# A mixture-of-experts block on one core: 280 tokens by dense products instead of 288, 104 tokens by gathered rows instead of 96

## The chip, the cores and the metric

The kernel runs on one NeuronCore of a Trainium2 chip. The metric is the device time of one execution in microseconds (us), taken as the median of several executions. A profile of one execution comes with it; its span runs from the first to the last instruction on the core.

The engines in the text: PE is the matrix engine (its weight loads are listed as PEld), DVE the vector engine, ACT the activation engine, POOL the general engine that here issues gathers and small copies, SP the engine that issues most loads. Each engine executes its own instructions in the order in which they stand, and waits on semaphores for the others.

## The reference

One transformer block on 512 tokens of width 2048: a mixer (chunked linear memory, forgetting attention, gated merge), cross attention over 256 memory rows, and an expert layer, each followed by a residual and a layer norm. The change lies in the expert layer:

```
q = (x @ w_pq).reshape(B, S, PEER_HEADS, 2, PEER_DK // 2)
sc = jnp.einsum('bshpd,hpnd->bshpn', q, sub_keys)          # 128 keys per half
top_s, top_i = lax.top_k(sc, PEER_TOPK)                    # 16 per half
best_s, best_pos = lax.top_k(cand_s, PEER_TOPK)            # 16 of the 256 pairs, per head
idx, g = take_along_axis(cand_i, best_pos), softmax(best_s)
# per token: 8 heads x 16 = 128 experts out of 16384
a = einsum('tkd,td->tk', expert_u[idx], x);  hact = gelu(a) * g
out = einsum('tk,tkd->td', hact, expert_v[idx])
x = layer_norm(DN_ALPHA * x + out, ln_w[2], ln_b[2])
```

An expert's number is 128 times its key in the first half plus its key in the second. So the 16384 experts are 128 groups ("keys") of 128.

## The kernel before, in words

All products are made in float32 accuracy from three products of split operands: a tile `w` becomes `whi` (a cast on ACT, L133) and `wlo = w - whi` (a subtraction on DVE, L134), and `whi*xhi + whi*xlo + wlo*xhi` are summed in PSUM (`products`, L201). Every weight tile of 128 x 1024 floats is loaded by SP (`load_raw`, L145), cast and subtracted. Two rings of buffers hold them in the expert layer, together six raw tiles, five `whi` and five `wlo`.

The mixer, the cross attention and the queries come first and are not changed. Token block 0 (128 tokens) has its experts done by gathering from an earlier point on. The blocks 1 to 3 are divided: the first 288 of their 384 tokens are dense, the last 96 gathered.

Dense tokens. For each key `c` of 128, `stage_a(c)` multiplies the 128 experts' `u` rows of that key with all dense tokens (two weight tiles, 48 products with 288 columns each) and applies gelu on ACT (tile `ga`). For each group of eight keys (`c0`, `J = 8`), `stage_o(c0, q)`, q = 0 to 3, multiplies the gated activations with the `v` rows of these keys (sixteen weight tiles a group, 24 products each, four PSUM banks `po`), and DVE adds the banks to `acc` (L1422). Between the two, `stage_h(c)` multiplies `ga` by the gate tile `G` (L1313) and splits the result into `hph` and `hpl`.

The gates are dense too: `G` says for every expert of a key and every token what weight the token gives it, mostly zero. It is built ahead in rounds of four tokens ("gate rounds" below): DVE makes two one-hot tiles `o` (L1244), ACT scales one of them token by token (four instructions, L1249), PE multiplies them (four products, L1250), and ACT copies the bank into four `stage` tiles (four copies, L1253). After 12 rounds (`GB = 48` tokens) the stage tiles are written to DRAM (`gd`, four DMAs issued by ACT, L1255). There are 72 rounds. `stage_h` reads `G` back for four keys at a time, so the first `stage_o` cannot begin before the last round is in DRAM. The rounds themselves wait for the selection of the top 16 (`select`, DVE).

`LOOK = 76` keys of `stage_a` run before the first `stage_o`; the other 52 are spread evenly over the groups. 126 of the 128 activations go to DRAM (`gad`, ACT queue) and come back (`gb`, SP queue); the text of the code calls them `spilled`.

Gathered tokens. `gathered(t, r0, n, ...)` takes n tokens; each holds 128/n partition rows, so that 128 experts are fetched at a time: n gathers from `u`, each followed by a product with the token's row and a sum (L929, DVE), then gelu and gates, then n gathers from `v`, each followed by a multiply-add into `xacc` (L932, DVE). A product with a 0/1 matrix folds the 128/n rows of a token (four products and copies, L950, L951). Each step is a job; `EARLY = 44` of the 194 jobs run beside the first 76 keys, the others at an even rate up to the group of key 112. A job waits for a given weight tile's split (`after`, "pace"). Each part ends with its own layer norm: two broadcast loads of norm weights, statistics, `rstd`, four DVE instructions (L964 to L983).

The end. In the last group, after each q, PE turns `acc` into token rows (`turned_out`, L1358), statistics are gathered, and after q = 3 `last_rows` finishes the norm of three blocks of dense tokens (128, 128 and 32) and writes them.

The order of instructions on each engine is not as written: a scheduler with a model of the durations lays it out when the program is built, and the built order of any version can be read. PE therefore has gate rounds, `stage_a` and `stage_o` interleaved in an order that is fixed before it runs.

## Time and profile before

| | us |
|---|---|
| median of three runs | 4829.66 |
| lowest and highest | 4826.51, 4833.37 |
| profiled execution | 4827.06 |
| its span | 4825.3 |
| PE busy | 4695.9 |
| DVE busy | 3736.9 |
| ACT busy | 2203.7 |
| first `stage_a` product | 3065.2 |
| first and last gate product | 3363.1, 3581.6 |
| first `stage_o` product | 3617.7 |
| last `stage_o` product | 4804.7 |

A row of a group or a timeline gives the source line, the engine, the operation, what is written from what and the tile's shape; in brackets or behind a bar stands how long the engine was idle before it and what ended that. "PE 120.00 (x906)" in a table of stretches means 120.00 us busy and 906 instructions that touch the stretch.

### The profile page before, as it was taken

To read this page: it belongs to the slowest core of one execution; us is meant where nothing else is said; L and a number is where in the kernel's file an instruction comes from. 1 tells how busy PE (TensorE), PEld (TensorE's weight loads), DVE (VectorE), ACT (ScalarE), POOL (GpSimd) and SP (SyncE) were. 2 spreads that over 40 slices of the span, in tenths; PEclk is the share of its full clock that TensorE was granted. 3 is DMA by queue.
4 is the path that set the end of the run, shared out by engine and by line. 5 is a ranking of instruction groups with operands and counts; after the bars stand their busy time and mean duration, and the time that the engine had idled before them with its cause. 6 is when DMAs were issued, how large, how long until landed. Compare 5 with 4: busy or idle time off the path is not lost. (4 is left out here: it accounts for less than half of the span.)

```text
span 4825.3 us, 75381 instructions
## 1 busy us (share of the span) xinstructions
PE 4695.9 (97%) x28720; PEld 4343.2 (90%) x28720; DVE 3736.9 (77%) x5326; ACT 2203.7 (46%) x3388; POOL 932.2 (19%) x884
## 2 busy tenths in 40 slices
PE   7999999999999899999989999999999999999999
PEld 6889788887888899999988779999999999999998
DVE  7776677766699777888769586899877888888886
ACT  6665666555543223343332334444874333343333
POOL 0000111200002332333334120111101222221110
PEclk9999999999999999999999999999999999999999
DMA  7888999865669899998889585588789999999993
GB/s 263 287 287 294 316 333 326 283 218 190 194 202 356 326 363 342 340 333 327 303 306 383 196 307 185 201 289 285 275 309 353 347 349 352 351 333 348 364 360 121
DMA packets 384380, 1435.00 MB, mean 297 GB/s; under 512 B 44412, under 2 KB 109676, under 8 KB 325392
## 3 DMA queue, kind: packets, MB, share of 16 engines
q1 hardware_dynamic: 268176, 832.52, 49.2%
q0 software_dynamic: 91456, 556.10, 30.8%
q10 hardware_dynamic: 24384, 41.56, 2.3%
q8 instruction: 225, 3.69, 0.3%
q14 instruction: 139, 1.14, 0.1%
HBM read 1338.10 MB, written 91.76 MB: 296 GB/s over the span
## 5 line engine op out<-in xcount | busy, mean ns | idle before, releaser
L134 DVE TENSOR_TENSOR wlo<-raw,whi 128x1024 fp32r<-128x1024 f32 x1472 | 1782.0, 1220 | 746.3 <-ACT whi L133 512.9
L133 ACT CAST whi<-raw 128x1024 fp32r<-128x1024 f32 x1472 | 1527.9, 1052 | 1710.7 <-PE mm L201 878.0
L201 PE MATMUL po<-hph,whi 128*128 128x288 f32 x2048 | 551.2, 296 | 9.9 <-ACT whi L133 9.9
L201 PE MATMUL sm<-Ch,whi 128*128 128x288 f32 x2048 | 557.8, 298 | 2.4 <-ACT whi L133 1.3
L201 PE MATMUL sm<-Cl,whi 128*128 128x288 f32 x2048 | 556.7, 296 | 0.0
L201 PE MATMUL po<-hpl,whi 128*128 128x288 f32 x2048 | 551.0, 296 | 0.5 <-DVE hpl L134 0.5
L901 POOL DMA_INDIRECT rows<-in_peer_u,eid x224 | 324.1, 1447 | 1173.5 <-DVE rows L929 486.8
L932 DVE SCALAR_TENSOR_TENSOR xacc<-rows,dots,xacc 128x2048 f32<-128x2048 f32 x224 | 525.4, 2345 | 21.6 <-DMA rows<-in_peer_v,eid 20.1
L901 POOL DMA_INDIRECT rows<-in_peer_v,eid x224 | 369.4, 1649 | 872.4 <-DVE xacc L932 464.4
L929 DVE SCALAR_TENSOR_TENSOR rows<-rows,xacc 128x2048 f32<-128x2048 f32 x224 | 511.3, 2285 | 24.1 <-DMA rows<-in_peer_u,eid 23.2
L201 PE MATMUL mm<-xh,whi 128*128 128x384 f32 x1280 | 437.7, 344 | 7.2 <-ACT whi L133 4.2
L201 PE MATMUL mm<-xl,whi 128*128 128x384 f32 x1280 | 430.9, 338 | 0.0
L201 PEld LDWEIGHTS po<-hph,whi 128*128 128x128 f32 x2048 | 383.9, 189 | 12.0 <-ACT whi L133 11.1
L201 PEld LDWEIGHTS sm<-Ch,whi 128*128 128x128 f32 x2048 | 384.9, 188 | 4.1 <-ACT whi L133 2.4
L201 PEld LDWEIGHTS po<-hpl,whi 128*128 128x128 f32 x2048 | 383.8, 189 | 2.4 <-issue 1.7
L201 PEld LDWEIGHTS sm<-Cl,whi 128*128 128x128 f32 x2048 | 385.0, 188 | 0.0
L201 PE MATMUL po<-hph,wlo 128*128 128x288 f32 x2048 | 337.9, 297 | 2.6 <-DVE wlo L134 2.5
L201 PE MATMUL sm<-Ch,wlo 128*128 128x288 f32 x2048 | 327.4, 298 | 1.1 <-DVE wlo L134 1.0
L201 PEld LDWEIGHTS po<-hph,wlo 128*128 128x128 f32 x2048 | 294.1, 189 | 7.1 <-DVE wlo L134 5.3
L201 PEld LDWEIGHTS sm<-Ch,wlo 128*128 128x128 f32 x2048 | 288.5, 188 | 3.8 <-DVE wlo L134 2.8
L201 PE MATMUL mm<-xh,wlo 128*128 128x384 f32 x1280 | 255.1, 335 | 0.0
L201 PEld LDWEIGHTS mm<-xh,whi 128*128 128x128 f32 x1280 | 242.2, 189 | 14.3 <-ACT whi L133 4.5
(440 smaller groups left out, 8527.7 us busy)
## 6 DMA issues: line engine op xcount, KB each, us to landing
raw<-in_w_in SPq DMA_DIRECT2D x512, 512.0 KB
raw<-in_uT SPq DMA_DIRECT2D x256, 512.0 KB
raw<-in_vq SPq DMA_DIRECT2D x256, 512.0 KB
raw<-in_w_xkv SPq DMA_DIRECT2D x64, 512.0 KB
raw<-in_w_br_ml SPq DMA_DIRECT2D x64, 512.0 KB
raw<-in_w_br_fx SPq DMA_DIRECT2D x64, 512.0 KB
raw<-in_w_out SPq DMA_DIRECT2D x64, 512.0 KB
raw<-in_peer_wq SPq DMA_DIRECT2D x64, 512.0 KB
```

The source lines that it names most:

```text
L133: nc.scalar.copy(hi, src)
L134: return nc.vector.tensor_sub(lo, src, hi.bitcast(F32))
L201: nc.tensor.matmul(o, w if stat else x, x if stat else w, start=k == first and x is xh and not part, stop=k == last and part == 1)
L901: i = nc.gpsimd.indirect_dma_start(out=rows, out_offset=None, in_=I[table], in_offset=bass.IndirectOffsetOnAxis(ap=ei[:, k:k + 1], axis=0))
L929: after(nc.vector.scalar_tensor_tensor(rows, rows, 1.0, xacc, op0=ALU.mult, op1=ALU.mult, accum_out=dots[:, k:k + 1]), last())
L932: after(nc.vector.scalar_tensor_tensor(xacc, rows, dots[:, k:k + 1], xacc, op0=ALU.mult, op1=ALU.add), last())
```

## The change

Seven things go together.

1. `NDENSE` is 280: every product, gelu, gate, split and add of the dense stages has 280 columns instead of 288, and there are 70 gate rounds in five groups of 14 (`GB = 56`).
2. The gathered tokens are 104, in three parts of 64, 32 and 8. The third part brings 16 gathers with 16 DVE instructions, four folding products and copies, and, since each of its tokens has 16 partition rows, 32 small copies of indices and gates and 16 small loads of its token rows on POOL.
3. `LOOK` is 72 and `EARLY` 56: 56 jobs run beside the first 72 keys.
4. The other 56 keys of `stage_a` are no longer spread evenly. The groups of keys 0 to 56 do none; each group from key 64 to 112 does the eight keys of the next group, two beside each q, and `stage_h` of a key follows its `stage_a` at once.
5. The activations of these 56 keys stay in SBUF; 72 activations go through DRAM instead of 126.
6. The remaining 155 jobs run 6 or 7 to a group up to the group of key 56, and 16 or 17 to a group from key 64 to key 104. The last two groups have none.
7. The three gathered parts no longer make their own norm. Each writes its rows to DRAM (`yg`), they are read back as one tile of 104 rows, and `gathered_rows` makes one norm for them in the last group, after q = 1.

```diff
-NDENSE = 288
-GATHERED = ((64, 64), (32, 32))
-GB = 48
+NDENSE = 280
+GATHERED = ((64, 64), (32, 32), (24, 8))
+GB = 56
...
+            if keep is not None:
+                nc.gpsimd.dma_start(keep, xacc[:n])
+                yield True
+                return
             lw = fin_load(gat)
...
-        LOOK = 76
-        EARLY = 44
-        GA_N = 3
         J = 8
+        LOOK = 72
+        EARLY = 56
...
-            if c in spilled:
+            if c < LOOK:
                 nc.scalar.dma_start(gad[c], ga)
             else:
-                gas[c] = ga
+                fetched[c] = ga
...
         def stage_h(c):
             for f in range(c, min(c + 3, NC_)):
+                if f // 4 not in gates:
+                    gates[f // 4] = mn.tile(...)
+                    nc.sync.dma_start(gates[f // 4], gd[:, :, f:f + 4])
+                if f < LOOK and f not in fetched:
+                    fetched[f] = mn.tile([P, NDENSE], F32, tag="gb", bufs=4, name=nm("gb"))
+                    nc.sync.dma_start(fetched[f], gad[f])
...
-                if q == 3 and not last:
+                if q == 3 and c0 + J < LOOK:
                     for c in (c0 + J + 2 * m, c0 + J + 2 * m + 1):
                         stage_h(c)
...
+        def gathered_rows():
+            st, y = last_norm["st"], yw[NT]
+            for q in range(4):
+                nc.vector.bn_stats(st[:NG, NT, 6 * q:6 * q + 6], y[:NG, q * 512:(q + 1) * 512])
+            nc.vector.bn_aggr(st[:NG, NT, 24:26], st[:NG, NT, 0:24])
+            for q in range(4):
+                weighted(NT, q, y[:, q * 512:(q + 1) * 512])
+            last_rows(NT, NT + 1, None)
...
+                if q == 1:
+                    gathered_rows()
                 if q == 3:
-                    last_rows(rest)
+                    last_rows(0, NT, rest)
-        ahead = [min(NC_, LOOK + -(-c * (NC_ - LOOK) // (NC_ - J))) for c in range(NC_)]
-        spilled = {...}
-        for a in range(ahead[0]):
+        for a in range(LOOK):
             stage_a(a)
             while done * LOOK < a * EARLY:
                 next(jobs, None)
                 done += 1
-        turn_g = [0]
+        room = [4 if c0 < LOOK - J else 10 for c0 in range(0, NC_ - 2 * J, J) for _ in range(2 * J)]
+        TOTAL, passed = sum(room), [0, 0]
         for c0 in range(0, NC_, J):
             def fill(i, c0=c0):
-                if i % 2:
-                    c = c0 + i // 2
-                    ...
-                    for a in range(ahead[c], ahead[c + 1] if c + 1 < NC_ else NC_):
-                        stage_a(a)
+                if i % 2 and LOOK <= c0 + J < NC_:
+                    a = c0 + J + i // 2
+                    stage_a(a)
+                    stage_h(a)
+                if room:
+                    passed[0] += room.pop(0)
+                    while passed[1] < njobs - EARLY and passed[1] * TOTAL <= passed[0] * (njobs - EARLY):
+                        next(jobs, None)
+                        passed[1] += 1
```

More of the change, by code (lines that the diff above doesn't have):

```diff
@@ L871, in query @@
                 yield (g,)
-        eid = cp.tile([P, 1 + len(GATHERED), P], I32, tag="eid", name="eid")
-        egg = cp.tile([P, 1 + len(GATHERED), P], F32, tag="egg", name="egg")
+        ecols, at_col = [], 0
+        for n in [P] + [n for _, n in GATHERED]:
+            ecols.append(slice(at_col, at_col + n))
+            at_col += n
+        eid = cp.tile([P, at_col], I32, tag="eid", name="eid")
+        egg = cp.tile([P, at_col], F32, tag="egg", name="egg")
         def rows_of(tp, sel, parts):
@@ L881, in rows_of @@
             if parts[0][2] == P:
-                nc.vector.tensor_copy(eid[:, parts[0][0]], ef)
-                nc.vector.tensor_copy(egg[:, parts[0][0]], sel["g"])
+                nc.vector.tensor_copy(eid[:, ecols[0]], ef)
+                nc.vector.tensor_copy(egg[:, ecols[0]], sel["g"])
                 return
@@ L904, in gather_rows, with gathered @@
             return rows
-        def gathered(t, r0, n, i, last, lag):
-            ei, gg = eid[:, i], egg[:, i]
+        def gathered(t, r0, n, i, last, lag, keep=None):
+            ei, gg = eid[:, ecols[i]], egg[:, ecols[i]]
             xacc = gat.tile([P, D], F32, tag="xacc", bufs=1, name=nm("xacc"))
@@ L1316, in stage_h @@
             hs[c] = (a, b)
-        jobs = chain(*(gathered(TB - 1, r0, n, 1 + i, lambda: work["last"], 1) for i, (r0, n) in enumerate(GATHERED)))
         NT = -(-NDENSE // P)
+        FIRST, NG = NDENSE % P, P - NDENSE % P
+        yg = dp.tile([NG, D], F32, tag="yg", name="yg")
+        jobs = chain(*(gathered(TB - 1, r0, n, 1 + i, lambda: work["last"], 1, yg[r0 - FIRST:r0 - FIRST + n])
+                       for i, (r0, n) in enumerate(GATHERED)))
         yw, last_norm = {}, {}
```

73 lines of the change are left out of this document (30 added, 43 removed).

## The prediction

> **What bounds the kernel now.** I read the page first, then a table of stretches around the expert layer, then the waits of PE in it, then the timelines where one stage passes into the next.
>
> ```profile
> span 4825.3 us, 75381 instructions
> PE 4695.9 (97%) x28720; PEld 4343.2 (90%) x28720; DVE 3736.9 (77%) x5326; ACT 2203.7 (46%) x3388; POOL 932.2 (19%) x884
> ```
>
> The table of stretches gives, per stretch, each engine's busy time and instructions, PE's granted clock, the share of the DMA engines and what they moved:
>
> ```profile
> core 0: us, PE busy (x) PEld busy (x) DVE busy (x) ACT busy (x) POOL busy (x), PEclk, DMA share, GB/s
> 467.00:476.00 9.00, 9.00 (x77) 9.00 (x76) 5.49 (x8) 3.14 (x3) 2.13 (x4) 1.00 0.85 284
> 1700.00:1890.00 190.00, 190.00 (x1098) 190.00 (x1097) 141.03 (x128) 53.05 (x58) 57.95 (x49) 1.00 0.94 355
> 3240.00:3360.00 120.00, 120.00 (x906) 120.00 (x905) 116.55 (x266) 50.02 (x59) 17.51 (x12) 1.00 0.86 293
> 3065.20:3617.70 552.50, 550.69 (x4234) 549.73 (x4235) 483.15 (x952) 328.57 (x819) 79.86 (x57) 1.00 0.81 285
> 3103.80:3309.50 205.70, 204.87 (x1543) 204.40 (x1543) 198.88 (x459) 82.41 (x100) 38.48 (x21) 1.00 0.87 302
> 3360.00:3582.40 222.40, 221.42 (x1758) 220.93 (x1757) 177.18 (x225) 190.41 (x651) 23.01 (x14) 1.00 0.77 273
> 3617.70:4804.70 1187.00, 1170.84 (x8693) 1156.36 (x8692) 966.55 (x1114) 448.16 (x568) 239.44 (x163) 1.00 0.89 331
> 4300.00:4400.00 100.00, 99.50 (x750) 99.03 (x749) 86.91 (x109) 37.63 (x47) 18.82 (x16) 1.00 0.99 377
> 4804.70:4825.30 20.60, 10.01 (x30) 4.16 (x28) 14.68 (x34) 0.60 (x2) 0.00 (x0) 0.61 0.31 115
> ```
>
> From the first dense product (3065.2) to the last (4804.7) PE is busy all but 18 us, so what the dense stages cost is the number of products times their pace. The pace is a stretch of one shape divided by its count, less the one or two products cut at the edges: 256 columns 9.00/75 = 120 ns (the first row, a stretch of 256-column products), 384 columns 190/1098 = 173.0 ns, 288 columns 120/906 = 132.5 ns. Two engines are near their limit beside PE: DVE, 198.9 of 205.7 us while it selects, and the DMA engines, share 0.99 at 377 GB/s at the height.
>
> **The pace.** From 256 to 288 columns the pace rises by 12.5/32 = 0.39 ns a column, from 288 to 384 by 40.5/96 = 0.42. Eight columns fewer are worth 3.1 to 3.4 ns; I take 3.3, so 129.2 ns. There are 6144 products in `stage_a` and 6144 in `stage_o`: 12288 x 3.3 ns = 40.6 us less, of which 11.4 us fall into the first 3456 products and 29.1 into the others.
>
> **Where the gate rounds stand.** The built order says more than the diff. Before, the first of 72 gate rounds stands on PE after 46.5 keys and the last after 70.4 of 76; over five keys follow it. After the change the first of 70 rounds stands after 54.9 keys, round 42 just before the end of key 72, and rounds 43 to 70 come with no dense product beside them; only then does `stage_o` begin. ACT cannot run ahead: the gelu of the 72nd key stands before round 43 in ACT's order, and it waits for that key's last product. The rounds start later since DVE is full before them (row 3103.8) and now has twelve more jobs in fewer keys there.
>
> ```profile
> L134 DVE TENSOR_TENSOR wlo<-raw,whi 128x1024 fp32r<-128x1024 f32 x1472 | 1782.0, 1220 | 746.3 <-ACT whi L133 512.9
> L932 DVE SCALAR_TENSOR_TENSOR xacc<-rows,dots,xacc 128x2048 f32<-128x2048 f32 x224 | 525.4, 2345 | 21.6 <-DMA rows<-in_peer_v,eid 20.1
> L929 DVE SCALAR_TENSOR_TENSOR rows<-rows,xacc 128x2048 f32<-128x2048 f32 x224 | 511.3, 2285 | 24.1 <-DMA rows<-in_peer_u,eid 23.2
> L1249 ACT ACTIVATE o<-o,gT 128x128 f32<-128x128 f32 x288 | 94.3, 424 | 19.6 <-DVE o L1244 16.4 <-issue 3.2
> L1422 DVE TENSOR_TENSOR acc<-acc,po 128x288 f32<-128x288 f32 x240 | 94.2, 448 | 91.7 <-PE po L201 91.7
> L1313 DVE TENSOR_TENSOR gb<-gb,G 128x288 f32<-128x288 f32 x126 | 54.1, 451 | 2.8 <-DMA gb<-gad 2.7
> L134 DVE TENSOR_TENSOR hpl<-gb,hph 128x288 fp32r<-128x288 f32 x126 | 54.0, 451 | 7.1 <-PE po L201 3.9 <-ACT hph L133 2.5 <-issue 0.5
> ```
>
> What a lone round costs is ACT's: in ACT's timeline four copies take 3537.66 to 3538.27 and four scalings 3538.27 to 3539.45, together 1.79 us. DMA issues stand on ACT as well: at a group's end the four writes of the stage tiles hold it 3.5 us once (3545.67 to 3549.15), 5.4 us the other time (the second fence, later in the same timeline).
>
> ```profile
> 3537.66 0.82 ACT L1253 COPY stage<-po 128x128 f32<-128x128 f32 x4
> 3538.27 1.37 ACT L1249 ACTIVATE o<-o,gT 128x128 f32<-128x128 f32 x4
> 3539.45 1.12 ACT L133 CAST whi<-raw 128x1024 fp32r<-128x1024 f32 x1
> ...
> 3545.67 0.33 ACTq L1255 DMA_DIRECT2D gd<-stage  x1
> ...
> 3546.04 3.11 ACTq L1255 DMA_DIRECT2D gd<-stage  x3
> 3549.20 1.28 ACT L1249 ACTIVATE o<-o,gT 128x128 f32<-128x128 f32 x4 [3.05 <-DVE o L1244]
> ```
>
> ```profile
> 3582.18 0.33 ACTq L1255 DMA_DIRECT2D gd<-stage  x1
> ...
> 3582.55 5.01 ACTq L1255 DMA_DIRECT2D gd<-stage  x3
> ```
>
> Behind the last round comes the way through DRAM. Before, SP issued the first read of `G` at 3594.83, 12.7 us after the first of the last four writes (3582.18), and the first gate multiply ran at 3605.32:
>
> ```profile
> 3594.83 0.61 SPq L1295 DMA_DIRECT2D G<-gd  x1
> ```
>
> ```profile
> 3605.32 0.82 DVE L1313 TENSOR_TENSOR ga<-ga,G 128x288 f32<-128x288 f32 x2
> ```
>
> That cost nothing then, since PE had `stage_a` until 3617.7. It has nothing now.
>
> **The first part, step by step.** Before: 3648 x 132.5 ns = 483.4; the busy 550.7 less that and 1 us of turns leaves 66.3 for 288 gate products, 0.23 us each. After: 3456 x 129.2 = 446.5, 168 gate products 38.6, turns and waits 1.5, sum 486.6. The jobs ahead: 12 more at 2.3 us (L929) are 28 us on a full DVE, against which the rounds move back by 8.4 keys; what reaches PE I bound by 0 (the split tiles lie up to five ahead, 5 x 3.2 = 16 us) and 10 (47 keys at the 6.43 us a key of row 3103.8, 32 keys, against PE's 48 x 0.1292 = 6.20), and take 2, near the lower end because the five tiles cover it. `stage_a` ends at 3065.2 + 488.6 = 3553.8.
>
> The 44 small copies ahead of the first gather, 12 before, cost POOL 16 us more:
>
> ```profile
> 3094.01 3.13 POOL L890 DMA_DIRECT2D egg<-sel_g  x6 [163.79 <-DVE v L811]
> ```
>
> Six take 3.1 us. The built order puts the first job behind them, later on DVE, so nothing waits; at worst 16 us of DVE's slack. The third part's 16 row loads stand on POOL between jobs and cost 8 us of an engine busy 239 of 1187.
>
> **The uncovered stretch.** After key 72: gelu, copies and five DMA issues 6 us; 28 rounds x 1.79 = 50.1; four issues at the group's end between 4.5; waits for stage tiles still being written and for DVE's one-hots 5 (one such wait was 3.05); four writes to landing 10.5 (four tiles of 0.9 MB at the 355 GB/s of row 1700, near the 12.7 seen); read of `G` 4, gate, cast and first products 3. Sum 83 us. Bounds: 66 with no wait and half of the DRAM way; 100 with 2.4 us a round. `stage_o` begins at 3637, 19 us later than before, though PE has four keys less behind it.
>
> At this place the Trainium skill, "TensorE: Matmul & The Clock Gate", Part 1 (The HAM clock gate), says that PE's clock halves after an idle window of about 3.4 us and comes back after as long a busy one. By that page gate products at half clock would take 1.84 us a round, so PE would pace it instead of ACT, and the sum would be about 6 us higher. The last row of stretches (clock 0.61 while PE is busy 10 of 20.6 us) agrees.
>
> **The second part.** Before, 8640 products x 132.5 = 1144.8 of 1187.0: 42.2 us besides. They include:
>
> ```profile
> PE po L201 <- ACT whi L133: 9.9, 5, 2.0
> PE po L201 <- DVE wlo L134: 2.5, 9, 0.6
> ```
>
> ```profile
> 3946.50 0.41 ACT L1283 ACTIVATE ga<-sm 128x288 f32<-128x288 f32 x1 [13.23 <-PE sm L201]
> ```
>
> ```profile
> 4696.33 0.29 PE L201 MATMUL po<-hph,whi 128*128 128x288 f32 x1
> 4696.56 1.04 PE L950 MATMUL fo<-xacc,fold 128*32 128x512 f32 x2
> 4697.53 0.40 PE L201 MATMUL po<-hpl,whi 128*128 128x288 f32 x1
> ```
>
> The five waits of 2.0 us are one pattern: in ACT's order a gelu, which waits for the key's last product, stands ahead of the cast of the weights that PE needs next. The built order has five such places before and one after; one fold copy that stands ahead of a cast is new. So 3 x 2.0 = 6 us go, with some 3 us of half clock that follow them. A fold costs 4697.53 - 4696.33 - 0.13 = 1.07 us, four more 4.3. The norm of 104 rows adds one turn and four products, 1.5, and 9 us of DVE work in a group where DVE has room; the two norms that go were off PE. Left: 42.2 - 6 - 3 + 4.3 + 1.5 = 39.0. After: 8832 x 129.2 = 1141.1 + 39.0 = 1180.1, so the last product ends at 4817.
>
> DVE there: a group without `stage_a` has 16 splits at 1.21 (1782.0/1472), 8 keys of gate and split at 0.43 each, 16 adds at 0.39 and seven jobs at 2.3, 48.6 us of PE's 384 x 0.1292 = 49.6; it fits, with 1 us to spare. A mixed group has 90 of 99. Keeping 54 activations out of DRAM takes 16 MB from the queues, and 16 gathers put 17 MB on: no change in sum.
>
> **The sum.** 3637 + 1180.1 + 20.6 for the same end + 0.5 for the DVE work in the last group = 4838 of span, 12.6 above 4825.3. The profiled execution took 4827.06, the median is 2.6 above it; the forecast for the median is 4829.66 + 12.6 = 4842. A difference under about 0.2% (9.7 us) cannot be told from none here.
>
> **Rivals.**
> - *Second half runs free* (faster). If the 39 us besides the pace in the second part are late transfers and misplaced casts that the new order removes, down to 12 folds and the norm (14.4), the time is 4842 - 24.6 = 4817. It decides from 22 us besides down. For it: four of five places go. Against it: the remaining waits of 0.4 to 0.6 us for `wlo` have no reason to go.
> - *Short stretch* (same). 66 instead of 83 us: 4825. For it: the DMA queues are empty then. Against: the 3.05 us wait for DVE, the 12.7 us to the read.
> - *Half clock in the stretch* (slower). Rounds paced by PE: 4848. For it: the clock row of the end.
> - *DMA as bound* (slower). Up to the group of key 104, weights (320 x 0.52 MB), 152 gathers (1.05), gates and activations sum to 359 MB for 7680 products; at PE's pace, 992 us, that is 362 GB/s. If the queues hold only 352, it takes 1019: 4869. For it: the mean of the second part is 331. Against: 377 with PE 99.5% busy. By the Trainium skill, "Perfetto Trace Analysis", Roofline, a lone core's 16 engines reach about 435 GB/s, and this would not occur; the row of 377 at a share of 0.99 puts the ceiling lower, and the row decides.
> - *The pace does not fall* with eight columns (the change does not do its work): 4842 + 40.6 = 4883. Against: three shapes on one line.
>
> **How the numbers follow.** Forecast 0.48 (its own range 4831 to 4856, a third of it within 0.2%), second half free 0.15, short stretch 0.08, half clock 0.12, DMA 0.13, pace 0.04. Faster 0.15; same 0.15 + 0.08 = 0.23; slower 0.33 + 0.12 + 0.13 + 0.04 = 0.62. The range 4817 to 4870 leaves out half of the free second half, the pace case and half of the DMA case, 0.18.
>
> **What would show it.** PE paced at 129 ns in dense stretches; a stretch of 75 to 90 us after the 72nd key in which PE has only gate products and then nothing, with ACT scaling and copying at 1.8 us a round; the first `stage_o` product near 3637; 36 to 42 us besides the pace after it; `stage_a` ending near 3554. A first `stage_o` product before 3620 or less than 22 us besides would make it wrong on the fast side; DMA shares of 0.99 with PE waiting for loads, on the slow side.

## The result, and the profile after

The changed kernel takes 4839.64 us (median of 15 runs, 4834.14 to 4849.36) against 4828.26 us before (15 runs, 4816.24 to 4833.37): by the ratio of the runs 1.0028 times as long, interval 1.0020 to 1.0035 (the two medians alone give 1.0024). That is slower by 0.28%, a small difference, but the interval lies above 1. The prediction said 4842 us, range 4817 to 4870, and gave "slower" a chance of 0.62. The sum came out within 2.4 us of the median; its parts did not. The second part began earlier than forecast and took longer, and the two cancelled.

The head of the page of the changed kernel:

```profile
span 4837.9 us, 75306 instructions
PE 4664.7 (96%) x28717; PEld 4310.1 (89%) x28717; DVE 3763.8 (78%) x5357; ACT 2201.0 (45%) x3374; POOL 931.0 (19%) x948
```

PE has 31 us less to do than before and the span is 12.6 us longer. The table of stretches of the changed kernel (columns as in the prediction: each engine's busy time, PE's clock, the DMA engines' share, GB/s) shows where the time stands. The rows are the 72 early keys, a dense stretch in them, what lies between the last early `stage_a` product and the first `stage_o` product, the gate rounds in it, a part of these, the eight groups without `stage_a`, and the whole second part:

```profile
3065.60:3547.40 481.80, 481.80 (x3792) 481.80 (x3793) 461.30 (x897) 260.62 (x559) 98.35 (x102) 1.00 0.88 318
3240.00:3360.00 120.00, 120.00 (x938) 120.00 (x938) 119.86 (x239) 47.74 (x59) 20.55 (x19) 1.00 0.96 355
3547.40:3624.20 76.80, 40.77 (x236) 36.15 (x234) 39.16 (x65) 54.18 (x233) 0.00 (x0) 0.82 0.47 184
3553.40:3608.30 54.90, 39.88 (x227) 35.45 (x227) 33.82 (x55) 51.26 (x222) 0.00 (x0) 0.88 0.32 130
3567.00:3582.00 15.00, 11.40 (x72) 9.87 (x71) 11.13 (x21) 15.00 (x67) 0.00 (x0) 1.00 0.05 21
3624.20:4024.00 399.80, 389.19 (x2944) 385.79 (x2945) 347.60 (x430) 158.12 (x204) 61.33 (x52) 0.98 0.93 345
3624.20:4817.20 1193.00, 1169.62 (x8899) 1151.04 (x8899) 976.51 (x1138) 461.34 (x584) 229.12 (x182) 0.99 0.87 320
```

The pace is 120 us / 937 = 128.1 ns in the dense row; the mean distance of two neighbouring products that do not wait is 128.8 ns in the whole second part (132.6 before). DVE is busy 119.9 of 120 us in the dense row, in which it selects and multiplies for the jobs, and PE does not wait for it there.

In the stretch of 76.8 us no dense product runs. The timeline of ACT shows its beginning, its middle and its end; the second fence is the read that follows on SP, the third PE's first product:

```profile
3549.10 4.25 ACTq L1264 DMA_DIRECT2D gd<-stage  x4
3553.40 2.45 ACT L1258 ACTIVATE o<-o,gT 128x128 f32<-128x128 f32 x8 [4.10 <-issue]
...
3568.01 1.43 ACT L1258 ACTIVATE o<-o,gT 128x128 f32<-128x128 f32 x4
3569.19 0.91 ACT L1262 COPY stage<-po 128x128 f32<-128x128 f32 x4
3569.81 1.46 ACT L1258 ACTIVATE o<-o,gT 128x128 f32<-128x128 f32 x4
...
3608.34 0.33 ACTq L1264 DMA_DIRECT2D gd<-stage  x1
```

```profile
3618.70 0.61 SPq L1302 DMA_DIRECT2D G<-gd  x1
```

```profile
3624.17 1.30 PE L201 MATMUL po<-hph,whi 128*128 128x280 f32 x4 [16.16 <-ACT hph L133]
```

Four steps fill it: 6.0 us of DMA issues and copies on ACT up to 3553.4; 54.9 us of rounds, one every 1.80 us (3568.01 to 3569.81), up to 3608.3; 10.4 us until the gates can be read back; 5.5 us until the first product.

The waits of PE in the second part of the changed kernel (total, times, longest). The first row holds the 16.2 us that end the stretch; the table of before stands in the prediction in part, with 9.9 us for `whi` as its largest row:

```profile
PE po L201 <- ACT hph L133: 19.8, 4, 16.2
PE po L201 <- DVE hpl L134: 4.7, 3, 3.5
PE fo L955 <- ACT xacc L956: 3.3, 5, 0.7
PE po L201 <- DVE wlo L134: 3.0, 2, 2.8
PE po L201 <- DVE acc L1436: 2.9, 4, 1.0
PE po L201 <- ACT whi L133: 1.6, 2, 1.4
```

The waits for `whi` nearly went, as forecast. Waits for the split activations (`hpl`, `hph`), for `wlo`, for `acc` and around the folding products came in their place. Those between dense products stand mostly in the eight groups without `stage_a`; the folds stand in later groups.

Two of the longest show where they come from. Ahead of the 3.5 us for `hpl`, which end at 3691.8, DVE had stood idle for 4.3 us until an activation was back from DRAM (first row). Ahead of the 2.8 us for `wlo`, which end at 4554.2, DVE had no idle time: a multiply-add of a job stands in its order ahead of the split that PE needs (the other two rows).

```profile
3687.23 0.45 DVE L1308 TENSOR_TENSOR gb<-gb,G 128x280 f32<-128x280 f32 x1 [4.26 <-DMA gb<-gad]
...
4550.68 2.35 DVE L937 SCALAR_TENSOR_TENSOR xacc<-rows,dots,xacc 128x2048 f32<-128x2048 f32 x1
4552.94 2.35 DVE L134 TENSOR_TENSOR wlo<-raw,whi 128x1024 fp32r<-128x1024 f32 x2
```

### The profile page after: what moved, and what is told of

It is laid out like the page before. It is cut to its first block, busy times and chain, and to the rows that moved or that the text cites. A ratio compares the mean times of both kernels' runs of the same rounds, so it can differ in the third digit from the quotient of the medians.

```text
span 4837.9 us, 75306 instructions
## 1 busy us (share of the span) xinstructions
PE 4664.7 (96%) x28717; PEld 4310.1 (89%) x28717; DVE 3763.8 (78%) x5357; ACT 2201.0 (45%) x3374; POOL 931.0 (19%) x948
## 3 DMA queue, kind: packets, MB, share of 16 engines
q1 hardware_dynamic: 256153, 823.27, 48.6%
## 5 line engine op out<-in xcount | busy, mean ns | idle before, releaser
L937 DVE SCALAR_TENSOR_TENSOR xacc<-rows,dots,xacc 128x2048 f32<-128x2048 f32 x232 | 544.5, 2347 | 28.3 <-DMA rows<-in_peer_v,eid 27.3
L201 PE MATMUL po<-hph,whi 128*128 128x280 f32 x2048 | 533.1, 294 | 24.2 <-ACT hph L133 19.8
L934 DVE SCALAR_TENSOR_TENSOR rows<-rows,xacc 128x2048 f32<-128x2048 f32 x232 | 529.9, 2287 | 31.5 <-DMA rows<-in_peer_u,eid 31.0
L201 PE MATMUL sm<-Ch,whi 128*128 128x280 f32 x2048 | 540.4, 294 | 1.6 <-ACT xacc L956 1.3
L201 PE MATMUL sm<-Cl,whi 128*128 128x280 f32 x2048 | 539.9, 293 | 0.0
L201 PE MATMUL po<-hpl,whi 128*128 128x280 f32 x2048 | 532.0, 293 | 4.7 <-DVE hpl L134 4.7
L906 POOL DMA_INDIRECT rows<-in_peer_v,eid x232 | 351.0, 1513 | 948.6 <-DVE wlo L134 465.2
L201 PE MATMUL po<-hph,wlo 128*128 128x280 f32 x2048 | 336.1, 293 | 3.0 <-DVE wlo L134 3.0
L201 PE MATMUL sm<-Ch,wlo 128*128 128x280 f32 x2048 | 311.9, 293 | 1.3 <-DVE wlo L134 1.3
```

The costliest lines, as they stand in the source:

```text
L201: nc.tensor.matmul(o, w if stat else x, x if stat else w, start=k == first and x is xh and not part, stop=k == last and part == 1)
L906: i = nc.gpsimd.indirect_dma_start(out=rows, out_offset=None, in_=I[table], in_offset=bass.IndirectOffsetOnAxis(ap=ei[:, k:k + 1], axis=0))
L934: after(nc.vector.scalar_tensor_tensor(rows, rows, 1.0, xacc, op0=ALU.mult, op1=ALU.mult, accum_out=dots[:, k:k + 1]), last())
L937: after(nc.vector.scalar_tensor_tensor(xacc, rows, dots[:, k:k + 1], xacc, op0=ALU.mult, op1=ALU.add), last())
```

## The experiments

Two theories stood at the start: that the uncovered gate rounds alone cost the time, so that covering them brings some 70 us; and as rival that the second part is bound by DVE or by the DMA queues and gives back what is gained ahead of it.

All runs in one table. "Ahead" is the number of keys and of jobs ahead; "bare" is the time between the last early `stage_a` product and the first `stage_o` product, "second" the time from there to the last `stage_o` product. "Besides" is what the second part takes besides products times pace, and it is divided into the time around folding products, around turns and norms, and the rest, which are waits between dense products and half clock behind them. "Share" is DVE's busy time in the second part over products times pace. All of these are worked out from the starts of instructions in the traces. The ratio is to the kernel before, run beside each version; two versions are best compared by their ratios. e5, e6 and e9 leave out part of the computation and are probes, not versions.

| run | ahead | us | ratio (interval) | bare | second | besides = folds + turns + rest | share |
|---|---|---|---|---|---|---|---|
| before | 76, 44 | 4828.26 | 1 | 0 | 1187.3 | 41.7 = 9.7 + 5.8 + 26.1 | 0.844 |
| after | 72, 56 | 4839.64 | 1.0028 (1.0020-1.0035) | 76.8 | 1193.0 | 55.5 = 18.4 + 8.3 + 28.7 | 0.858 |
| e1 | 72, 30 | 4881.93 | 1.0109 (1.0086-1.0131) | 0 | 1283.8 | 146.2 = 73.5 + 8.3 + 64.4 | 0.913 |
| e2 | 88, 64 | 4825.09 | 0.9992 (0.9982-1.0001) | 0 | 1133.4 | 94.8 = 35.1 + 8.3 + 51.4 | 0.894 |
| e3 | 76, 44 | 4861.95 | 1.0071 (1.0054-1.0087) | 0 | 1227.5 | 114.6 = 31.3 + 6.2 + 77.1 | 0.901 |
| e4 | 72, 56 | 4865.93 | 1.0078 (1.0060-1.0097) | 80.6 | 1199.0 | 27.9 = 9.7 + 7.6 + 10.6 | 0.806 |
| e5 | 72, 56 | 4795.60 | 0.9927 (0.9911-0.9944) | 8.6 | 1191.5 | 54.0 = 27.1 + 8.3 + 18.5 | 0.725 |
| e6 | 72, 56 | 4977.58 | 1.0290 (1.0247-1.0333) | 77.9 | 1329.4 | 191.8 = 23.5 + 8.3 + 160.0 | 0.857 |
| e7 | 96, 80 | 4811.74 | 0.9969 (0.9957-0.9980) | 0 | 1067.0 | 77.8 = 16.9 + 8.3 + 52.6 | 0.880 |
| e8 | 88, 76 | 4824.43 | 0.9986 (0.9976-0.9995) | 24.3 | 1097.6 | 58.9 = 15.6 + 8.3 + 35.0 | 0.862 |
| e9 | 72, 56 | 4831.17 | 0.9999 (0.9989-1.0008) | 65.8 | 1194.3 | 56.7 = 18.4 + 8.3 + 29.9 | 0.859 |
| e10 | 72, 56 | 4853.06 | 1.0049 (1.0035-1.0063) | 76.7 | 1205.3 | 67.8 = 29.5 + 6.0 + 32.3 | 0.871 |
| e11 | 96, 88 | 4820.51 | 0.9978 (0.9969-0.9988) | 1.9 | 1053.1 | 63.9 = 14.8 + 8.3 + 40.8 | 0.871 |
| e12 | 104, 88 | 4812.70 | 0.9966 (0.9954-0.9979) | 0 | 1011.6 | 71.8 = 15.6 + 8.3 + 47.9 | 0.884 |

**e1, fewer jobs ahead of the gate rounds.**

```diff
-        EARLY = 56
+        EARLY = 30
```

> The changed kernel with EARLY = 30 instead of 56: 30 gathered jobs run beside the first 72 keys, the other 181 later, spread by the same rule (7 or 8 to a group up to key 56, 19 or 20 from key 64 to key 104). In the built order the first gate round then stands after 44.2 keys of stage_a (54.9 in the changed kernel), the last after 66.1, and none is left behind the 72nd key (29 in the changed kernel). Theory (the gate rounds without a dense product beside them cost the time): the 76.8 us between the last early stage_a product and the first stage_o product fall to under 8; stage_a ends near 3550, stage_o begins near 3555, and if the second part stays at its 1193 us the time is about 4771 us. Adding 26 jobs there at 2.3 us of DVE, of which some 2 us a group have no room in the eight groups without stage_a, 4785; range 4765 to 4800. Rival (the second part is bound by DVE and the DMA queues, and gives it all back): first stage_o near 3555 as well, but the second part grows by 60 to 70 us, 4830 to 4840. Rival (the stretch is due to something else than the jobs ahead of the rounds): the stretch stays over 60 us and the time near 4840.

The bare stretch went, and the kernel became 39 us slower than the changed one by the ratios. The order of the rounds is therefore set by the jobs ahead of them, as the theory has it, but the second part took it all back and more. Two things were wrong. First, `stage_o` began at 3580, not 3555: the rounds that moved in among the dense products bring their own gate products with them (29 rounds at some 0.92 us, 27 us), so covering the stretch is worth 558.6 - 509.6 = 49 us of the first part and not 77. Second, the second part grew by 91 us. PE's waits there:

```profile
PE fo L955 <- DVE xacc L937: 47.2, 2, 33.0
PE po L201 <- ACT hph L133: 24.8, 12, 2.9
PE po L201 <- DVE wlo L134: 11.1, 6, 3.3
```

A folding product has a fixed place in PE's order, and behind it stand dense products that do not need it. At 4605 PE reached it while DVE had ten multiply-adds of that part left. The timeline of DVE:

```profile
4606.36 7.12 DVE L937 SCALAR_TENSOR_TENSOR xacc<-rows,dots,xacc 128x2048 f32<-128x2048 f32 x3
4616.45 2.35 DVE L937 SCALAR_TENSOR_TENSOR xacc<-rows,dots,xacc 128x2048 f32<-128x2048 f32 x1 [2.97 <-DMA rows<-in_peer_v,eid]
4619.07 2.35 DVE L937 SCALAR_TENSOR_TENSOR xacc<-rows,dots,xacc 128x2048 f32<-128x2048 f32 x1 [0.27 <-DMA rows<-in_peer_v,eid]
```

They went through at 3.2 us each, three row buffers deep, with PE idle for 33 us.

**e2, more keys as cover.**

```diff
-        LOOK = 72
-        EARLY = 56
+        LOOK = 88
+        EARLY = 64
```

> The changed kernel with LOOK = 88 and EARLY = 64: 16 keys of stage_a more stand ahead of the first stage_o, as cover for the gate rounds, with 64 jobs beside them (0.73 a key, 0.78 in the changed kernel) and 147 later. In the built order the rounds stand between 55.6 and 82.5 keys, none behind the 88th key. Theory: nothing is uncovered; 88 keys end near 3547 + 16 x 6.2 = 3646, stage_o begins within 5 us of that, and the second part has 16 keys (99 us) fewer: 1193 - 99 = 1094, last product near 4745, time about 4767 us, range 4755 to 4785. Rival (the second part is bound by DVE or by transfers, since its jobs crowd into eleven groups without stage_a): it loses 20 us or more there, 4790 to 4840, with DVE above 47 of 49.6 us in each of those groups and PE waiting for wlo or hpl.

The rival's case, in the middle of its 4790 to 4840, though not in every sign: DVE is at 47 us or more in six of the eleven groups without `stage_a`, not in each, and PE's longest wait is that of a fold (14.2 us). Nothing is bare any more: the first part is 607.6 us for 88 keys, 50 us less than the changed kernel's 558.6 plus 16 keys at 6.2. The second part is 95 us above its pace instead of 55 and gives 39 of the 50 back.

**e3 and e4, the size without the order and the order without the size.**

The first diff is against the kernel before, the second against the changed kernel. The first is shown without the packed index tiles, which e3 has like the changed kernel.

```diff
-NDENSE = 288
-GATHERED = ((64, 64), (32, 32))
-GB = 48
+NDENSE = 280
+GATHERED = ((64, 64), (32, 32), (24, 8))
+GB = 56
...
```

> The kernel before with the split alone: 280 dense tokens, gathered parts of 64, 32 and 8, gate groups of 56 tokens (and the index tiles packed as in the changed kernel, for room). LOOK = 76, EARLY = 44, the even spread of the later keys, the activations in DRAM and a norm for each part stay. In the built order the gate rounds stand between 44.3 and 67.6 keys of 76. Theory (eight columns are worth their pace, and what loses the gain is the order, not the size): 12288 products at 128.8 instead of 132.6 ns save 46.7 us; four more folds and a third norm cost 4 to 8, 17 more jobs 0 to 10 on DVE and the queues; 4828 - 46.7 + 10 = 4791 us, range 4780 to 4805. Rival (the third part's 16 gathers, its small copies or its own norm eat the gain): 4815 to 4840.

```diff
-NDENSE = 280
-GATHERED = ((64, 64), (32, 32), (24, 8))
-GB = 56
+NDENSE = 288
+GATHERED = ((64, 64), (32, 32))
+GB = 48
```

> The changed kernel with the split of before: 288 dense tokens, gathered parts of 64 and 32, gate groups of 48; LOOK = 72, EARLY = 56 (138 jobs later), the later keys a group ahead and in SBUF, and the single norm stay. In the built order the rounds start after 57.4 keys, and 32 of 72 stand behind the 72nd key. Theory (size and order add up): 12288 products at 3.8 ns more, +46.7; 32 instead of 29 uncovered rounds, +5; four folds and 17 jobs fewer, -5 to -15; 4839.6 + 42 = 4881 us, range 4870 to 4892, with a stretch of 80 to 85 us without dense products. Rival (the pace of the eight columns does not reach the time in this order since other engines bound it): 4840 to 4855.

Both expectations missed, and together they say most. By the ratios to before, the smaller size costs 34 us with the order of before (1.0071), and saves 24 with the new order (1.0028 against 1.0078). The new order costs 38 us with the old size, and saves 21 with the new. So whether either half pays depends on the other. In e3 the pace fell as it should (33 us less for 8640 products), and the waits rose by more. Its PE waits in the second part:

```profile
PE po L201 <- ACT whi L133: 21.9, 12, 4.4
PE fo L954 <- DVE xacc L936: 10.0, 1, 10.0
PE po L201 <- DVE wlo L134: 8.5, 9, 2.2
```

PE waits for a cast twelve times instead of five, and one fold waits 10 us. In e4, where PE has more and DVE less to do, the rest of the waits is 10.6 us, the least of all.

After these four, "besides" stood in the same order as DVE's share (0.806, 0.844, 0.858, 0.894, 0.901, 0.913), and that became the theory for the next runs. The rival was the DMA queues, whose bytes go roughly the same way.

**e5 and e6, half of DVE's work on the jobs, and half of their bytes.**

```diff
-                    after(nc.vector.scalar_tensor_tensor(rows, rows, 1.0, xacc, ...
+                    h = slice(0, D // 2 if n < P else D)
+                    after(nc.vector.scalar_tensor_tensor(rows[:, h], rows[:, h], 1.0, xacc[:, h], ...
...
-                    after(nc.vector.scalar_tensor_tensor(xacc, rows, dots[:, k:k + 1], xacc,
+                    after(nc.vector.scalar_tensor_tensor(xacc[:, h], rows[:, h], dots[:, k:k + 1], xacc[:, h],
```

> The changed kernel in which the 208 jobs of the gathered tokens of the last block do their multiply on DVE over 1024 of the 2048 columns (the other half of these tokens' dot products and sums is left out, so the output of the 104 tokens is wrong); every gather, DMA and product stays. Theory (DVE's share of the stretch decides, in both parts): 208 x 1.15 = 239 us of DVE go. In the built order the first gate round then stands after 39.3 keys and the last after 67.6, none behind the 72nd: the stretch of 76.8 us falls under 10, and with DVE at 976 - 150 x 1.15 = 803 us of 1138 (0.71, against 0.858) the excess of the second part over its pace falls from 55 to 20 to 35 us; 4839.6 - 70 - 27 = 4743 us, range 4730 to 4765. Rival (the DMA queues bound the second part, 381 MB at 0.87 busy): the stretch goes all the same, but the second part, with the same bytes in the same time, keeps 55 us or gets more; 4770 to 4790.

```diff
-            i = nc.gpsimd.indirect_dma_start(out=rows, out_offset=None, in_=I[table],
-                                             in_offset=bass.IndirectOffsetOnAxis(ap=ei[:, k:k + 1], axis=0))
+            i = nc.gpsimd.indirect_dma_start(out=rows[:h], out_offset=None, in_=I[table],
+                                             in_offset=bass.IndirectOffsetOnAxis(ap=ei[:h, k:k + 1], axis=0))
...
                 next(jobs, None)
                 done += 1
+        rows_now[0] = P // 2
```

> The changed kernel in which the 155 later jobs gather 64 instead of 128 rows each and work on 64 partitions (half of the experts of these tokens is left out, so the output of the 104 tokens is wrong); DVE instructions keep their 2048 columns, so their time stays, and some 150 x 0.52 = 78 MB of 381 go from the second part's transfers. The first part is the same: 29 gate rounds behind the 72nd key, a stretch of 75 to 80 us, stage_o from 3624. Theory (DVE's share): the second part stays within 15 us of its 1193, excess 40 to 65; 4825 to 4845 us. Rival (the DMA queues bound it): the excess falls to 20 to 30 us, 4805 to 4815.

e5 took 4795.6 us, above the theory's range and the rival's. It confirmed the first half of the theory: with DVE free of 208 half multiplies the rounds come early and the bare stretch falls to 8.6 us; of the 68 us 41 remain in the first part, for the reason found in e1. The second part did not follow: 54.0 us besides, which is what the rival of the DMA queues had named. The rest fell by a third, from 28.7 to 18.5, but the folds rose from 18.4 to 27.1, among them one wait of 4.7 us for the last multiply-add. So with half of DVE's work on the jobs the waits between products were fewer, and the folds cost no less. Which of this is load and which the new order was not separated.

e6 cannot decide what it was made for, and shows something else. The bytes fell (column GB/s, 320 in the changed kernel), and the kernel became some 127 us slower than the changed one by the ratios (138 between the medians):

```profile
3624.00:4953.00 1329.00, 1213.34 (x8896) 1184.76 (x8897) 974.73 (x1138) 465.66 (x584) 297.05 (x182) 0.95 0.83 228
```

DVE's waits in e6, and the transfers of the gathers in e6 and then in the changed kernel, with the median time to landing at the end:

```profile
DVE xacc L942 <- DMA rows<-in_peer_v,eid: 142.1, 56, 8.1
```

```profile
rows<-in_peer_v,eid POOLq DMA_INDIRECT x104, 10.0
```

```profile
rows<-in_peer_v,eid POOLq DMA_INDIRECT x104, 9.3
```

A gather of 64 rows took as long to land here as one of 128. Each multiply stands closer to its gather all the same: 10.9 us from issue to multiply in the median of the second part's 150 jobs, 15.1 in the changed kernel, 17.4 before. DVE then stands still for rows that are not there, and PE behind it. A likely reason is that the planner took the smaller gathers to be shorter; its model was not read. Whether the queues' bytes bound the second part stays open from this run; the groups shown at e12 speak against it.

**e7 and e8, more cover, with more jobs in it.**

```diff
-        LOOK = 72
-        EARLY = 56
+        LOOK = 96
+        EARLY = 80
```

> The changed kernel with LOOK = 96 and EARLY = 80 (0.83 jobs a key ahead; 131 later). In the built order the gate rounds stand between 54.3 and 85.1 of 96 keys. The second part has 7296 - 768 = 6528 products, pace 841 us; DVE there loses 24 splits pairs (24 x 2 x 1.2 = 58 us), 24 keys' gelu gates stay, and 24 jobs (55 us): 976 - 113 = 863?; counted by products and jobs, share 0.99 of the pace. Theory (the excess grows with DVE's share: 0.806 gave 28 us, 0.858 55, 0.894 95, 0.901 115, 0.913 146): stage_o begins near 3720 with nothing uncovered, but the second part loses over 150 us: 4840 to 4900. Rival (only misplaced single waits cost, whatever the share): excess 40 to 60, 4770 to 4790.

```diff
-        LOOK = 72
-        EARLY = 56
+        LOOK = 88
+        EARLY = 76
```

> The changed kernel with LOOK = 88 and EARLY = 76 (0.86 a key ahead; 135 later), against e2 with 64 early jobs. The rounds stand between 54.3 and 87.2 of 88 keys. Twelve jobs (28 us of DVE) move from the second part (e2: 928 of 1039 us, 0.894) into the first. Theory (share of DVE): second part 900 of 1039, 0.867, excess 60 to 70 instead of 95, but the last rounds end at the 87th key, so 15 to 25 us of the way through DRAM are uncovered again, and the first part, fuller by 28 us, ends 0 to 10 us later: 4805 to 4830 us. Rival (the excess is not a matter of load but of where single products stand): 4825 plus 20, 4840 or more.

The expectation of e7 counted its second part wrong: it has 6144 + 32 x 48 = 7680 products (989 us), not 6528, so DVE's share is 0.880 and not 0.99. At 0.880 the series that the expectation gives asks for a value between 55 and 95, and 77.8 us were measured; but that was not forecast. The time of 4811.7 us is faster than both kernels. e8 came close to what was expected in each part: share 0.862 (0.867), 58.9 us besides (60 to 70), and a bare stretch of 24.3 us, since the last round stands at the 87th key. In it PE does nothing, and its clock is halved in most of it:

```profile
3689.00:3713.30 24.30, 0.00 (x0) 0.00 (x0) 7.93 (x7) 1.97 (x5) 1.68 (x1) 0.57 0.86 345
```

This is the way through DRAM. From the first of the last four writes, in ACT's timeline, to the first `stage_o` product at 3713.3 it is 28.8 us with weights in the queues beside it; in the changed kernel it was 15.9 (3608.3 to 3624.2) with the queues empty when it began, and 17.5 were forecast:

```profile
3684.53 0.33 ACTq L1264 DMA_DIRECT2D gd<-stage  x1
```

**e9, what paces the lone rounds.**

```diff
-                    nc.scalar.activation(o0[:, u], o0[:, u], AF.Copy, scale=selT["g"][:, c])
+                    if hb < 3:
+                        nc.scalar.activation(o0[:, u], o0[:, u], AF.Copy, scale=selT["g"][:, c])
```

> The changed kernel without ACT's four scalings in the last two of the five gate groups (rounds 43 to 70; the gate values of 112 dense tokens are left out, so the output is wrong there). In the built order 29 rounds stand behind the 72nd key as before. Theory (ACT paces the lone rounds, 4 scalings at 0.293 and 4 copies at 0.157 us, 1.82 us a round in the profile of the changed kernel): a round falls to DVE's two one-hots, 1.3 us, 28 x 0.52 = 15 us less, the stretch 62 us instead of 76.8, time 4825 us, range 4815 to 4832. Rival (PE at half clock paces them: eight records of a round at half speed are about 1.8 us): the stretch stays 74 to 79 us, and so does the time, 4835 to 4848.

The bare stretch fell by 11 us, to 65.8, and the time by 8.5 us between the medians (14 by the ratios). ACT paces the rounds in the changed kernel. Without its scalings some rounds wait for `stage` tiles still being written, so that not all of the 15 us came. The timeline of ACT in e9, with the idle time now ahead of each set of copies:

```profile
3564.37 0.94 ACT L1263 COPY stage<-po 128x128 f32<-128x128 f32 x5 [0.91 <-DMA gd<-stage]
3566.80 0.78 ACT L1263 COPY stage<-po 128x128 f32<-128x128 f32 x4 [1.48 <-PE po L1260]
```

The rival, PE at half clock, falls: in the changed kernel's row from 3567 to 3582 the granted clock is 1.00 although PE is idle for a quarter of it. Over the whole section of the rounds it is 0.88: it fell twice for 6.8 us, behind waits of PE of 5.6 and 3.5 us. The second of these, in the changed kernel:

```profile
3592.37 6.53 PE L1259 MATMUL po<-o,o 128*128 128x128 f32 x32 [3.47 <-ACT stage L1262]
```

The records that start at half clock stand 213 ns apart, so a round of eight takes PE 1.70 us there, still less than ACT's 1.80.

**e10, the norms of the parts back.**

```diff
...
-            yw[NT] = gat.tile([P, D], F32, tag="xacc", bufs=1, name="yw_g")
-            nc.gpsimd.dma_start(yw[NT][:NG], yg)
...
-                if q == 1:
-                    gathered_rows()
```

> The changed kernel with the norm of before: each of the three gathered parts makes its own norm and writes its rows, and the one norm for 104 rows in the last group is gone. The first part and the gate rounds are as in the changed kernel (29 behind the 72nd key). Theory (the norms lie beside PE): on PE one turn and four products of 0.2 to 0.6 us go, 2.5 us (turns and norms of the last group cost 8.3 us in the changed kernel, 5.8 before); three norms put 3 x 9 us of work on DVE in groups where it is 0.84 busy; 4836 us, range 4828 to 4846. Rival (work added to DVE there makes PE wait, and moves single products to worse places): 4855 to 4880.

Between the two expectations: 4853.1 us, by the ratios 10 us slower than the changed kernel (1.0049 against 1.0028). Turns and norms cost 2.3 us less, as forecast, and the folds 11 us more; one of them now waits for DVE, the second row of PE's waits in the second part:

```profile
PE po L201 <- ACT hph L133: 19.8, 4, 16.2
PE fo L955 <- DVE xacc L937: 7.0, 1, 7.0
```

**e11 and e12, whether fewer jobs or more groups without `stage_a` decide.**

```diff
-        LOOK = 72
-        EARLY = 56
+        LOOK = 96
+        EARLY = 88
```

> The changed kernel with LOOK = 96 and EARLY = 88, against e7 with 80 early jobs (4811.7 us). The gate rounds stand between 54.3 and 87.9 of 96 keys, so eight keys, 49 us, cover the way through DRAM. Eight jobs (18 us of DVE) move into the first part, where DVE was busy 603 of 662 us, out of the second (870 of 1067). Theory (fewer jobs a group in the groups without stage_a, 6.6 instead of 7.1, mean fewer waits there): excess of the second part 55 to 65 instead of 77.8 us, first part 0 to 8 us longer, 4802 us, range 4793 to 4812. Rival (the waits come from where the built order puts single instructions, not from the load): any place within 25 us around 4812, as likely above as below.

```diff
-        LOOK = 72
-        EARLY = 56
+        LOOK = 104
+        EARLY = 88
```

> The changed kernel with LOOK = 104 and EARLY = 88: 0.85 jobs a key ahead, 123 later, 7.2 to a group in twelve groups without stage_a. The gate rounds stand between 54.3 and 88.0 of 104 keys. The total of products is the same as in e7; nothing was uncovered there. Theory (load in the groups without stage_a): as e7 within 10 us, 4812, range 4802 to 4822: the first part 49 us longer, the second 49 us shorter, its excess 70 to 85 us again. Rival (the DMA queues bound the groups without stage_a, 0.94 busy, and there are now twelve of sixteen of them): excess 100 us or more, 4835 and up.

In e11 the second part does what the theory says (63.9 us besides, expected 55 to 65), and the first part loses it again: 685.1 us instead of e7's 662.4, where 0 to 8 us more were expected. So the 4820.5 us lie outside the theory's range. The largest row of PE's waits in e11 is new:

```profile
PE sm L201 <- ACT whi L133: 10.6, 1, 10.6
```

Ahead of that cast in ACT's order stands a gelu whose tile was still being written to DRAM:

```profile
3716.88 0.41 ACT L1291 ACTIVATE ga<-sm 128x280 f32<-128x280 f32 x1 [13.26 <-DMA gad<-ga]
```

e12 came where the theory put it, at 4812.7 us with 71.8 us besides; the rival of the DMA queues had asked for 100 or more. As a test of the queues that is weak, since e7 has eleven groups without `stage_a` and e12 twelve. The groups one by one say more. Here are two of the changed kernel, those of key 8 and of key 32:

```profile
3675.30:3730.00 54.70, 51.23 (x386) 50.96 (x385) 44.95 (x56) 21.82 (x29) 7.55 (x8) 0.97 0.91 338
3832.00:3882.50 50.50, 49.81 (x386) 49.58 (x386) 47.14 (x60) 19.58 (x25) 10.34 (x8) 1.00 0.98 374
```

Each has 384 products, 49.5 us at the pace. The group in which the DMA engines moved most loses 1 us, the other 5. In the traces of the changed kernel and of those runs that keep its order and whole jobs there are 88 groups with neither `stage_a` nor a fold; the thirteen of them that moved 365 GB/s or more lose 1.4 us in the mean and none more than 4. So the bytes do not bound these groups. Single late transfers still cost, as the 4.3 us for an activation showed. By DVE's busy time over the pace the loss of a group is 1.8 us in the mean below 0.90, 2.5 from 0.90 to 0.95, 4.8 up to 1.00 and 7.4 above, with a wide spread at each: DVE is busier in the second of the two rows.

e7 and e12 are the fastest full versions, 0.3% faster than before and not told apart from each other.

## Why the prediction was right

Its direction and its sum were right; by its own steps:

- *The pace.* Expected 129.2 ns, measured 128.8: 46.7 instead of 40.6 us saved over 12288 products. Right, a little short.
- *The first part.* Expected to end at 3553.8, ended at 3547.4. Half of the 6.4 us is the pace (3456 x 0.4 ns = 1.4) and the 2 us set aside for a full DVE, which did not come, since PE did not wait while DVE was full (row 3240); the remainder lies in the gate products and turns.
- *The uncovered stretch.* Expected 83 us, bounds 66 and 100, measured 76.8. The steps hold one by one: 6 and 6.0 for the beginning; 1.79 and 1.80 a round; 10.5 and 10.4 to the read of `G`. The section of the rounds took 54.9 us where 59.6 were summed, and the end 5.5 where 7 were. The rounds behind the last key are what decides the sign; the prediction read 28 of them from the built order, and 29 ran there (232 of 560 gate records, eight to a round). The first `stage_o` product came at 3624.2, where 3637 was forecast.
- *What the stretch is worth.* The prediction compared starts of `stage_o` and needed no price for it, so it was not misled; the expectations of e1 and e5 were. Of 77 us bare, 41 to 50 are to be had, because the gate products have to run somewhere.
- *The second part.* Expected 39.0 us besides the pace, with 36 to 42 named as the sign, measured 55.5; this step failed. The five waits behind a gelu did go (9.9 us for `whi` became 1.6), and their half clock with them. But folds cost 18.4 us where 9.7 + 4.3 were expected, because five of them, three in a row, wait for ACT's copy of the bank (3.3 us of waits) and the dense products behind two of these wait as well (1.3 us); turns and norms cost 8.3 where 5.8 + 1.5 were. The rest, which was to fall from 26.1 by 9 us, rose to 28.7: other waits took the place of those that went. They stand mostly where six or seven jobs meet a group without `stage_a`: in the first 400 us of the second part PE loses 20 us to them and to the half clock behind them. The prediction's sum for DVE there, 48.6 of 49.6 us a group, was called a fit. DVE's busy time did fit (at most 47.5 us a group), and PE waited all the same: for a split behind a multiply-add in DVE's order, or for an activation that came late, as the two waits above show.
- *The norms.* Two norms that go were costed at nothing since they were off PE. Giving each part its norm back costs some 10 us (e10), most of it in the folds.
- *The rivals.* The half clock in the stretch falls to the clock rows and e9: the clock was full where the rounds idle 0.5 us at a time, it fell behind two longer waits (5.6 and 3.5 us), and even there a round took 1.70 us and not the 1.84 that the prediction reckoned. The 6 us that it put on this rival do not follow from its 1.84 us either: 28 rounds x 0.05 us are 1.4. By the Trainium skill, "TensorE: Matmul & The Clock Gate", Part 1 (The HAM clock gate), the clock falls after an idle window of some 3.4 us. These two waits agree with it, and so do the bare 24.3 us of e8 with their 0.57. The DMA bound falls: the second part ran at 320 GB/s, its waits are put down to DVE and ACT, and the groups that moved most lost little. The free second half falls with the 55.5 us. The short stretch was the nearest of them, 10 us away.

So the 12.6 us of span come about as follows. The first part is 6 us longer: 76.8 of bare stretch, less 25.5 for four keys, 13.1 of pace, 28 for the gate products that moved out from among the dense ones, and 4 of smaller things. The second is 6 us longer: 25.5 for the four keys, less 33.6 of pace, plus 13.8 besides. Against the forecast the stretch was shorter by 6.2, the keys ahead of it by 6.4, and the second part longer by 12.9: that the sum was met to 2.4 us owes much to luck.

What is behind the second part's waits is settled in part. Over the kernels with whole jobs the rest column rises with DVE's share (10.6 us at 0.806, 26 to 30 at 0.844 to 0.859, 32 to 53 at 0.862 to 0.894, 64 and 77 at 0.913 and 0.901), and halving DVE's work in the jobs lowered it by a third (e5). e6 has the share of the changed kernel (0.857) and a rest of 160.0, so a DVE that stands still for its rows cost more here than any share of busy time did. How much of the rest is load and how much placement was not separated: each edit builds a new order.

## What to carry to other kernels

When a tuned, statically ordered kernel gets less work on its bounding engine, look first at the engine that is second: here DVE's share was 0.84 before, 0.86 after the change and 0.91 with more jobs put beside the same products (e1), and what PE lost besides the pace was 42, 55 and 146 us. Work that must be finished before a stage can start (here the gates in DRAM) wants cover behind it as long as its last steps plus the way through memory, 16 us here with the queues empty and 29 with weights in them; read from the built order, not from the source, how many steps stand behind the last covering product, and price what it would win by the whole part, not by the hole. And change size and order together, testing both halves: each alone was a loss of 0.7 to 0.8%, both together one of 0.3%.

## What was not expected of the hardware

- The share of the DMA engines did not follow the bytes. The second part of e6 has a share of 0.83 at 228 GB/s, that of the changed kernel 0.87 at 320: halving the rows of the gathers left their landing time (10.0 and 9.3 us) and nearly all of the share. So a high share did not mean here that the bytes were at a limit; the prediction's rival of a DMA bound rested on such a row.
- Waits of PE between 1.8 and 2.5 us that began at full clock are followed by a stretch of half clock in 22 of 44 places in the second parts of the fourteen traces, waits of 3.5 us and more in 24 of 24. The stretches come in multiples of 3.4 us, behind the shorter waits mostly a single one (18 of 22), so a wait of 2 us costs nothing or, as a rule, 1.7 us more. The Trainium skill, "TensorE: Matmul & The Clock Gate", Part 1 (The HAM clock gate), names an idle window of about 3.4 us; the multiples agree, but waits well under that length were enough here in half of the places.
